# A bidirectional hybrid encoder on one core: sums of the twofold product moved to GpSimd, its first left operands split earlier, and a fixed order for the first matmuls

## The chip, the cores and the metric

The kernel runs on one core of one Trainium2 chip. The metric is the device time of one execution in microseconds. Three runs of the kernel before took 2148.56, 2149.13 and 2149.67 us, so the median is 2149.13 us. Engine names are those of the profile: PE is TensorE's matmul stream, PEld its weight loads, DVE is VectorE, ACT is ScalarE, POOL is GpSimd, SP is the sequencer that issues nearly all DMAs.

## What is computed

One encoder layer runs over 1,024 prompt tokens and 256 sample tokens, each with 16 meta tokens in front. All data are float32. Cut to what matters:

```python
u = rms_norm(h, norm_w) @ w_in            # 2048 -> 6656 columns: qa ka va za qb kb vb zb
ya = global_gqa(rope(norm(qa)), rope(norm(ka)), va) * silu(za)
yb = neighbourhood_attention(norm(qb), norm(kb), vb, rpb) * silu(zb)
y = concat([ya, yb]) @ w_out              # 2048 -> 2048
return h + y
```

## The kernel before

Every float32 product is made as three matmuls of split numbers. An operand is split into a high part, which ACT rounds (L72), and a low part, which DVE makes by subtracting the high part from the full number (L73). With high and low parts h and l, a product is h·h + h·l + l·h. The work has three stages: projection of a first token chunk (`chunk1`), projection and attention of the second (`chunk2`), and the output projection (`outproj`).

**The opening.** `strips` projects strips of 128 columns of `w_in`. The first call does three strips together: a key strip (j = 0), a value strip (j = 1) and a gate strip (j = 2, 496 columns where the others have 512). The contraction of 2,048 goes in 16 depth steps of 128, four of them to a chunk `c`. The list `OPENING` fixes for the first three chunks in which order inputs are loaded and split: a number is the x tile of a depth step (DMA L104, ACT L128, DVE L131), and a tuple is a strip's weights, or a range of depth steps of them, `(j, i, e)` (DMA L232, ACT L72, DVE L73). SP, ACT and DVE keep this order. The nine matmuls of a depth step (three products, lines L269, L270 and L271, for each strip) are only written in the order of the strips; the tile framework's scheduler places them on PE by its own estimate of when operands are ready. Ahead of them `chunk1` issues `WARM` matmuls on a zero tile (L692), on which nothing depends.

**The end of the attention and the output projection.** `outproj` makes the product with `w_out` by seven block products in place of eight. The first two, products 1 and 2, go in ten steps each: five token tiles t by two column halves, 24 matmuls a step (L1126 to L1128). In product 2 the step's result is added to a running tile by two DVE instructions, `o<-o,u` and `o<-o,pq` (L1136); the second reads PE's PSUM. The next block product is itself made by seven half-size products (`class Twice`): `GROUPS` lists 18 groups of 12 matmuls each (L1431), the first three for right operand "11" with token tiles 0, 1 and 4, the next three for "21", then t2, t3, t4, t1 and 22.

While PE does product 2, `Twice.ahead(n)` is called at each of its ten steps and prepares the first groups:

- `loads(2, n)` at steps 0 to 3 brings four tiles `ww` of 128x512 of each right operand, in the order "11", "21", "12", "22" (SP, L1093);
- `load_tile(t)` brings two tiles `yr` and `sum_tile(t)` adds them into `ysum` (128x1024, DVE, L1348);
- `weights(s)` makes the four sums of right operands t1 = 12 - 11, t2 = 22 - t1, t3 = 22 - 12 and t4 = 21 - t2, each as four DVE subtractions of 128x512 (L1348 too);
- `make(s)` splits right operands into `wm` (ACT L72, DVE L73); their slots are those of product 2's right operands, so each waits for PE to be done with the old one;
- `make_left(s, t)` splits a left operand into `yh` and `yl` (ACT L72, DVE L73).

From this stage on `in_order` ties each engine to the order in which the code is written, so a DVE or ACT instruction that waits holds all that stand behind it. In this order the splits of the first two left operands, ("11", 0) and ("11", 1), come last, at step 9, behind the splits `wm` of "11" and "21". POOL has no work after the attention.

Of the kernel before, what the change touches and what calls it, by code (L numbers as in the profile page):

```python
# [16 lines left out]
ALU = mybir.AluOpType  # L17
# [6 lines left out]
KT = 16  # L24
# [7 lines left out]
T1 = NMETA + NS + C1P  # L32
# [10 lines left out]
QB = 256  # L43
WIN0 = (0, 1, 3, 4)
HALF = 192
WARM = 7
WTYPE = (0, 1, 1, 2)
FILL = 1
LATE = 48
# [11 lines left out]
QA, KA, VA, ZA, QB_, KB, VB, ZB = 0, 8, 10, 12, 20, 28, 36, 44  # L61
# [4 lines left out]
class Kern:  # L66
# [146 lines left out]
    def strips(self, jobs, getx):  # L213


        nc, tc = self.nc, self.tc
        out = [[pool.tile([P, 512], F32, tag=tag, name="pp") for pool, tag in pools] for _, _, pools in jobs]
        for c in range(KT // WCH):
            behind = self.behind.pop(0) if self.behind else None
            ws = [None] * len(jobs)  # L220
# [29 lines left out]
            opening = self.projected == 3 and not self.second and c < len(OPENING)  # L250
# [4 lines left out]
                    piece(*o)  # L255
            nb = len(jobs[0][1])
            for b in range(nb)[::-1] if self.turn else range(nb):
                steps = [(j, c * WCH + k) for k in range(WCH) for j in range(len(jobs))]
                if self.projected > 50 and not self.second:
                    steps.sort()  # L260
                for j, kt in steps:
                    xh, xl = getx(kt)[b]
                    k, first, last = kt % WCH, kt == 0, kt == KT - 1
                    wh, wl, _ = ws[j]
                    p, n = out[j][b], jobs[j][1][b][1]
                    if (jobs[j][0], c) in self.wide:
                        n = T1
                    m = T1 if first and jobs[j][0] == QA + 2 and not self.second else n
                    nc.tensor.matmul(p[:, :m], wh[:, k, :], xh[:, :m], start=first, stop=False)  # L269
                    nc.tensor.matmul(p[:, :n], wh[:, k, :], xl[:, :n], start=False, stop=False)  # L270
                    self.lastmm = nc.tensor.matmul(p[:, :n], wl[:, k, :], xh[:, :n], start=False, stop=last).ins  # L271
# [395 lines left out]
                yield  # L667

    def chunk1(self):
        self.opening = [None, None]  # L670
# [666 lines left out]
class Twice:  # L1337
# [26 lines left out]
    def weights(self, s):  # L1364
# [40 lines left out]
    def ahead(self, n):  # L1405
        if n < 4:
            self.loads(2, n)
        for f, x in {2: [(self.load_tile, 0)], 3: [(self.load_tile, 1)], 4: [(self.sum_tile, 0)],
                     5: [(self.load_tile, 4), (self.sum_tile, 1), (self.weights, "t1")],
                     6: [(self.load_tile, 2), (self.weights, "t2")],  # L1410
                     7: [(self.sum_tile, 4), (self.load_tile, 3), (self.weights, "t3"), (self.weights, "t4")],
                     8: [(self.sum_tile, 2), (self.make, "11"), (self.make, "21")]}.get(n, ()):
# [168 lines left out]
```

## Time and profile before

| what | number |
|---|---|
| median of three runs | 2149.13 us |
| the profiled execution's own time | 2149.74 us |
| its span, first to last instruction | 2148.0 us |
| PE busy | 2139.4 us, 100% |
| DVE, ACT, POOL busy | 1699.2, 1218.5, 539.4 us |
| PE's waits for other engines, all added | 5.0 us |
| from the start of product 2's last step to its end | 1867.99 to 1873.4 us |
| groups of the twofold product | from 1873.4 us |

Times inside the execution count from the start of the span. A timeline row gives the start, the busy time, the engine, the line, the operation and its tiles, how many instructions the row merges (x4), and in brackets how long the engine had been idle before it and what ended that idle time. PE's ends are modelled: its matmuls overlap, so their rate is read from one start to the next. A window row gives each engine's busy time with its instruction count, then the granted TensorE clock (1.00 is full speed), the DMA share and the bytes moved.

### The profile page before, as it was taken

The numbers are of one execution on the slowest core, as the hardware profiler recorded it, in microseconds if no ns is written. First come the engines' busy times: TensorE is split into PE (matmuls) and PEld (weight loads), VectorE is DVE, ScalarE is ACT, GpSimd is POOL, SyncE is SP. The second block draws the span as 40 slices with busy tenths as digits, with TensorE's granted clock in tenths as the row PEclk, the third lists the DMA queues.
The fourth block names the chain that finished last, engine by engine and source line by source line (L and its number), as shares of the span: only waits on it lengthen the run. The fifth ranks groups of instructions, "written<-read, shape, count | busy, mean of one in ns | idle before, by whom it ended". The sixth has DMA issues, their size and how long they took to land.

```text
span 2148.0 us, 33409 instructions
## 1 busy us (share of the span) xinstructions
PE 2139.4 (100%) x11437; PEld 1862.2 (87%) x11437; DVE 1699.2 (79%) x3103; ACT 1218.5 (57%) x2470; POOL 539.4 (25%) x250
## 2 busy tenths in 40 slices
PE   9999999999999999999999999999999999999999
PEld 7888888888888889998998888999989988788887
DVE  7798877777874899898799888787787776686763
ACT  7777644555665777777677776444444454262230
POOL 1242422233221223232133413333333312000000
PEclk9999999999999999999999999999999999999999
DMA  8757799987654333334333333654434355852663
GB/s 295 224 184 227 246 319 308 338 280 265 213 187 131 101 104 113 102 106 125 101 103 101 106 119 126 209 161 137 131 128 125 115 193 183 288 163 97 235 225 108
DMA packets 257707, 377.21 MB, mean 176 GB/s; under 512 B 43104, under 2 KB 109184, under 8 KB 257536
## 3 DMA queue, kind: packets, MB, share of 16 engines
q1 hardware_dynamic: 256960, 374.80, 54.0%
q8 instruction: 90, 1.47, 0.3%
q14 instruction: 81, 0.66, 0.1%
q10 hardware_dynamic: 576, 0.27, 0.0%
HBM read 281.01 MB, written 100.38 MB: 178 GB/s over the span
## 4 chain that ended last, share of the span: by engine, by line
PE 97%; DVE 1%; DMA 1%; SPq 0%; issue 0%; ACT 0%; DVEq 0%; ACTq 0%
PE pp L271 22%; PE pp L269 22%; PE pp L270 22%; PE pq L1128 4%; PE pq L1126 4%; PE pq L1127 4%; PE po L464 3%; PE pq L1431 2%; PE po L564 2%; PE sp L530 2%; PE sp L424 2%; PE sp L425 2%; PE sp L426 2%; PE po L465 1%; PE tp L585 0%; DMA yl<-yd 0%
## 5 line engine op out<-in xcount | busy, mean ns | idle before, releaser
L269 PE MATMUL pp<-x,wh 128*128 128x512 f32 (+1 forms) x1664 | 651.3, 394 | 0.6 <-ACT wh L72 0.6
L271 PE MATMUL pp<-x,wl 128*128 128x512 f32 (+1 forms) x1664 | 647.3, 389 | 0.7 <-DVE wl L73 0.7
L270 PE MATMUL pp<-x,wh 128*128 128x512 f32 (+1 forms) x1664 | 646.7, 389 | 0.0
L271 PEld LDWEIGHTS pp<-x,wl 128*128 128x128 f32 x1664 | 312.4, 188 | 64.3 <-DVE wl L73 1.8
L269 PEld LDWEIGHTS pp<-x,wh 128*128 128x128 f32 x1664 | 312.6, 188 | 55.4 <-ACT wh L72 2.1
L270 PEld LDWEIGHTS pp<-x,wh 128*128 128x128 f32 x1664 | 312.7, 188 | 54.1 <-DVE x L131 0.3
L304 POOL PARTITION_ALL_REDUCE m<-ms x78 | 238.4, 3056 | 297.7 <-ACT ms L302 207.3
L388 POOL PARTITION_ALL_REDUCE tot<-a x80 | 182.1, 2276 | 462.4 <-DVE a L385 429.8
L73 DVE TENSOR_TENSOR wl<-wr,wh 128x512 fp32r<-128x512 f32 (+2 forms) x288 | 210.1, 734 | 89.1 <-ACT wh L72 68.5
L72 ACT CAST wh<-wr 128x512 fp32r<-128x512 f32 (+2 forms) x288 | 173.8, 609 | 166.4 <-PE pp L270 150.7
L270 PE MATMUL pp<-xb,wh 128*128 128x272 f32 x832 | 240.4, 289 | 0.0
L269 PE MATMUL pp<-xb,wh 128*128 128x272 f32 x832 | 239.5, 288 | 0.0
L271 PE MATMUL pp<-xb,wl 128*128 128x272 f32 x832 | 239.2, 288 | 0.0
L370 POOL PARTITION_ALL_REDUCE ma<-m x80 | 112.3, 1403 | 452.8 <-DVE m L368 439.8
L1126 PE MATMUL pq<-wm,yh 128*128 128x512 f32 x480 | 187.5, 391 | 0.0
L1127 PE MATMUL pq<-wm,yh 128*128 128x512 f32 x480 | 186.9, 389 | 0.0
L1128 PE MATMUL pq<-wm,yl 128*128 128x512 f32 x480 | 186.8, 389 | 0.0
L270 PEld LDWEIGHTS pp<-xb,wh 128*128 128x128 f32 x832 | 156.4, 188 | 8.5
L269 PEld LDWEIGHTS pp<-xb,wh 128*128 128x128 f32 x832 | 156.5, 188 | 8.1
L271 PEld LDWEIGHTS pp<-xb,wl 128*128 128x128 f32 x832 | 157.4, 189 | 0.9
L73 DVE TENSOR_TENSOR ph<-S,ph 128x512 fp32r<-128x512 f32 x136 | 101.7, 755 | 13.5 <-ACT ph L72 13.2
L1128 PEld LDWEIGHTS pq<-wm,yl 128*128 128x128 f32 x480 | 90.1, 188 | 18.7
(241 smaller groups left out, 3996.4 us busy)
## 6 DMA issues: line engine op xcount, KB each, us to landing
wr<-in_w_in SPq DMA_DIRECT2D x413, 256.0 KB, 3.5
wld<-wl SPq DMA_DIRECT2D x132, 256.0 KB, 4.3
wl<-wld SPq DMA_DIRECT2D x132, 256.0 KB, 3.2
yr<-yd SPq DMA_DIRECT2D x35, 512.0 KB, 4.8
wq<-in_w_out SPq DMA_DIRECT2D x64, 256.0 KB, 4.8
td<-wq SPq DMA_DIRECT2D x64, 256.0 KB, 3.3
ww<-td SPq DMA_DIRECT2D x64, 256.0 KB, 4.4
ww<-in_w_out SPq DMA_DIRECT2D x48, 256.0 KB, 4.7
```

Source lines behind the costliest of these rows:

```text
L72: self.hi = nc.scalar.copy(hi, full).ins
L73: return nc.vector.tensor_tensor(out=lo, in0=full, in1=hi.bitcast(F32), op=ALU.subtract).ins
L269: nc.tensor.matmul(p[:, :m], wh[:, k, :], xh[:, :m], start=first, stop=False)
L270: nc.tensor.matmul(p[:, :n], wh[:, k, :], xl[:, :n], start=False, stop=False)
L271: self.lastmm = nc.tensor.matmul(p[:, :n], wl[:, k, :], xh[:, :n], start=False, stop=last).ins
L304: nc.gpsimd.partition_all_reduce(m2[:], ms[:], P, RED.add)
L370: nc.gpsimd.partition_all_reduce(ma[:], m1[:], P, RED.max)
L388: nc.gpsimd.partition_all_reduce(tot[:], a1[:], P, RED.add)
L464: nc.tensor.matmul(po[:], vh, hl[:, i], start=j == 0, stop=False)
L1126: nc.tensor.matmul(ps, yh, wh, start=k == 0, stop=False)
L1127: nc.tensor.matmul(ps, yh, wl, start=False, stop=False)
L1128: self.lastmm = nc.tensor.matmul(ps, yl, wh, start=False, stop=k == 7).ins
```

## The change

Five edits:

1. `Twice.weights` issues its sixteen subtractions on GpSimd instead of VectorE.
2. `Twice.ahead` calls `make_left("11", 0)` and `make_left("11", 1)` at step 8, ahead of `sum_tile(2)` and of the splits of "11" and "21", instead of at step 9 behind them.
3. In the first chunk (c == 0) of the opening a list `FIRST` gives the order of the nine matmuls of a depth step as pairs (strip, product), one list for the first depth step and one for the next three, and each matmul is placed behind the one before.
4. `OPENING` takes the x tile of depth step 2 ahead of the second halves of the weights of strips 1 and 2.
5. `WARM` goes from 7 to 8.

```diff
-WARM = 7
+WARM = 8
-OPENING = ([0, (0, 0, 1), (1, 0, 2), (2, 0, 2), (0, 1, 2), 1, (0, 2, 4), (1, 2, 4), (2, 2, 4), 2, 3],
+OPENING = ([0, (0, 0, 1), (1, 0, 2), (2, 0, 2), (0, 1, 2), 1, (0, 2, 4), 2, (1, 2, 4), (2, 2, 4), 3],
+FIRST = [[(int(c), int(q)) for c, q in o.split()] for o in ("00 10 01 02 11 12 20 21 22", "00 10 20 01 02 11 12 21 22")]
@@ strips
-                steps = [(j, c * WCH + k) for k in range(WCH) for j in range(len(jobs))]
-                if self.projected > 50 and not self.second:
+                steps = [(j, c * WCH + k, (0, 1, 2)) for k in range(WCH) for j in range(len(jobs))]
+                if opening and c == 0:
+                    steps = [(j, k, (q,)) for k in range(WCH) for j, q in FIRST[k > 0]]
+                elif self.projected > 50 and not self.second:
                     steps.sort()
...
+                    for q in products:
...
+                        i = nc.tensor.matmul(out[j][b][:, :m], w[q // 2][:, k, :], x[q % 2][:, :m], start=first, stop=last).ins
+                        if opening and c == 0 and self.lastmm:
+                            self.place_after(i, self.lastmm, "in turn")
+                        self.lastmm = i
@@ Twice.weights
-            self.sub(out[i], self.raw[a][i], self.raw[b][i])
+            self.nc.gpsimd.tensor_tensor(out=out[i], in0=self.raw[a][i], in1=self.raw[b][i], op=ALU.subtract)
@@ Twice.ahead
-                     8: [(self.sum_tile, 2), (self.make, "11"), (self.make, "21")]}.get(n, ()):
-            f(x)
-        if n == 9:
-            self.make_left("11", 0)
-            self.make_left("11", 1)
+                      8: [(self.make_left, "11", 0), (self.make_left, "11", 1), (self.sum_tile, 2), (self.make, "11"), (self.make, "21")]}.get(n, ()):
+            f(*x)
```

All instructions outside these two places keep their order on every engine. Line numbers move by one to three: L269 to L271 become one line, L271, and L72, L73, L1136 and L1348 become L73, L74, L1139 and L1351.

On PE, at the start of the program, the names pp_347, pp_348 and pp_349 are the sums of strips 0, 1 and 2 in the kernel before, x_350 and x_374 the x tiles of depth steps 0 and 1 (high or low part), and wh and wl the weights' parts:

```order
L269 MATMUL pp_347<-x_350,wh_354 128x512
L269 MATMUL pp_348<-x_350,wh_359 128x512
L269 MATMUL pp_349<-x_350,wh_365 128x496
L270 MATMUL pp_347<-x_350,wh_354 128x512
L270 MATMUL pp_348<-x_350,wh_359 128x512
L270 MATMUL pp_349<-x_350,wh_365 128x496
L271 MATMUL pp_347<-x_350,wl_355 128x512
L271 MATMUL pp_348<-x_350,wl_360 128x512
L269 MATMUL pp_347<-x_374,wh_354 128x512
L269 MATMUL pp_348<-x_374,wh_359 128x512
L271 MATMUL pp_349<-x_350,wl_366 128x496
```

The same place now, where the strips' sums are pp_348, pp_349 and pp_350 and the x tiles x_351 and x_375:

```order
L271 MATMUL pp_348<-x_351,wh_355 128x512
L271 MATMUL pp_349<-x_351,wh_360 128x512
L271 MATMUL pp_348<-x_351,wh_355 128x512
L271 MATMUL pp_348<-x_351,wl_356 128x512
L271 MATMUL pp_349<-x_351,wh_360 128x512
L271 MATMUL pp_349<-x_351,wl_361 128x512
L271 MATMUL pp_350<-x_351,wh_366 128x496 x2
L271 MATMUL pp_350<-x_351,wl_367 128x496
L271 MATMUL pp_348<-x_375,wh_355 128x512
L271 MATMUL pp_349<-x_375,wh_360 128x512
```

Strip 2's first product, the third matmul before, now stands seventh; the four products of strips 0 and 1 with low parts have moved ahead of it. On SP the DMA of the x tile of depth step 2 has moved ahead of two weight DMAs (128x256 each); ACT and DVE each handle that x tile ahead of the second half of strip 1's weights.

On DVE, from step 7 of product 2 to the preparations for the third group, before:

```order
L1348 TENSOR_TENSOR ww<-ww 128x512 x4
L1348 TENSOR_TENSOR wt<-ww,v 128x512 x4
L1136 TENSOR_TENSOR o<-o,u 128x512
L1136 TENSOR_TENSOR o<-o,pq 128x512
L1348 TENSOR_TENSOR ysum<-yr 128x1024
L73 TENSOR_TENSOR wm<-ww,wm 128x512 x8
L1136 TENSOR_TENSOR o<-o,u 128x512
L1136 TENSOR_TENSOR o<-o,pq 128x512
L73 TENSOR_TENSOR yl<-ysum,yh 128x512 x2
L1136 TENSOR_TENSOR o<-o,u 128x512
L1136 TENSOR_TENSOR o<-o,pq 128x512
L73 TENSOR_TENSOR wm<-v,wm 128x512 x4
```

The same stretch now:

```order
L1139 TENSOR_TENSOR o<-o,u 128x512
L1139 TENSOR_TENSOR o<-o,pq 128x512
L74 TENSOR_TENSOR yl<-ysum,yh 128x512 x2
L1351 TENSOR_TENSOR ysum<-yr 128x1024
L74 TENSOR_TENSOR wm<-ww,wm 128x512 x8
L1139 TENSOR_TENSOR o<-o,u 128x512
L1139 TENSOR_TENSOR o<-o,pq 128x512
L1139 TENSOR_TENSOR o<-o,u 128x512
L1139 TENSOR_TENSOR o<-o,pq 128x512
L74 TENSOR_TENSOR wm<-v,wm 128x512 x4
```

The sums are gone from DVE (the first eight stand higher up in the same way), and the two `yl` of the first left operands stand ahead of `ysum` and of the eight `wm`. On ACT the two `yh` of those operands have moved ahead of the eight `wm` in the same way. On POOL, behind its last reduction of the attention, now stand one instruction that the order lists as `ISA` (L1378, with no wait; the same kind stands ahead of POOL's first select and its first reduction) and the sixteen subtractions, in the order t1, t2, t3, t4.

More of the change, by code (lines that the diff above doesn't have):

```diff
@@ L257, in strips @@
             for b in range(nb)[::-1] if self.turn else range(nb):
-                steps = [(j, c * WCH + k) for k in range(WCH) for j in range(len(jobs))]
-                if self.projected > 50 and not self.second:
+                steps = [(j, c * WCH + k, (0, 1, 2)) for k in range(WCH) for j in range(len(jobs))]
+                if opening and c == 0:
+                    steps = [(j, k, (q,)) for k in range(WCH) for j, q in FIRST[k > 0]]
+                elif self.projected > 50 and not self.second:
                     steps.sort()
[L261 to L271, printed above, removed]
+                for j, kt, products in steps:
+                    x = getx(kt)[b]
+                    k, w = kt % WCH, ws[j]
+                    n = T1 if (jobs[j][0], c) in self.wide else jobs[j][1][b][1]
+                    for q in products:
+                        first, last = kt == q == 0, kt == KT - 1 and q == 2
+                        m = T1 if first and jobs[j][0] == QA + 2 and not self.second else n
+                        i = nc.tensor.matmul(out[j][b][:, :m], w[q // 2][:, k, :], x[q % 2][:, :m], start=first, stop=last).ins
+                        if opening and c == 0 and self.lastmm:
+                            self.place_after(i, self.lastmm, "in turn")
+                        self.lastmm = i
                 if self.turned and (c, b) == self.tie:
```

10 lines of the change are left out of this document (5 added, 5 removed).

## The prediction

> **What bounds the kernel now.** I read the page's first line and PE's waits first.
>
> ```profile
> span 2148.0 us, 33409 instructions
> ```
>
> ```profile
> PE pq L1431 <- DVE yl L73: 2.5, 1, 2.5
> PE warm L692 <- DVE wz L689: 1.2, 1, 1.2
> PE pp L271 <- DVE wl L73: 0.7, 1, 0.7
> PE pp L269 <- ACT wh L72: 0.6, 2, 0.3
> ```
>
> PE is busy all the time but for four waits of 5.0 us together, in 2148 us. So this change, which takes no matmul away, can win little. Half of the waiting is one wait at the head of the twofold product, where the change works; the last row is the opening, where it works too. The timeline of PE and the windows around the first place come next.
>
> ```profile
> 1867.99 0.39 PE L1126 MATMUL pq<-wm,yh 128*128 128x512 f32 x1
> ...
> 1873.43 0.61 PE L1431 MATMUL pq<-wm,yh 128*128 128x512 f32 x2
> 1876.52 0.79 PE L1431 MATMUL pq<-wm,yl 128*128 128x512 f32 x1 [2.47 <-DVE yl L73]
> ...
> 1880.20 0.39 PE L1431 MATMUL pq<-wm,yl 128*128 128x512 f32 x1
> ```
>
> ```profile
> 1873.00:1876.50 3.50, 1.04 (x5) 0.54 (x3) 3.47 (x7) 0.00 (x0) 0.00 (x0) 0.99 0.86 291
> 1876.50:1880.20 3.70, 3.69 (x9) 2.94 (x10) 3.60 (x7) 0.00 (x0) 0.00 (x0) 0.55 0.91 295
> ```
>
> The last step of product 2 takes 24 matmuls from 1867.99 to 1873.43, which is 0.227 us each. Two matmuls of the twofold product follow, then PE is idle for 2.47 us. What the list of waits doesn't show stands in the second window: behind the wait the granted clock is 0.55, and from 1876.52 to 1880.20 nine matmuls take 3.68 us where nine at 0.227 take 2.04. The wait thus costs 2.47 + 1.64 = 4.11 us.
>
> Who made the wait stands in DVE's timeline.
>
> ```profile
> 1849.98 1.31 DVE L73 TENSOR_TENSOR yl<-yl,yh 128x512 fp32r<-128x512 f32 x2 [2.86 <-ACT yh L72]
> ...
> 1852.34 2.49 DVE L1348 TENSOR_TENSOR v<-ww 128x512 f32<-128x512 f32 x4
> ...
> 1864.69 2.49 DVE L1348 TENSOR_TENSOR wt<-ww,v 128x512 f32<-128x512 f32 x4
> ...
> 1869.63 4.90 DVE L73 TENSOR_TENSOR wm<-ww,wm 128x512 fp32r<-128x512 f32 x8
> ...
> 1875.78 1.28 DVE L73 TENSOR_TENSOR yl<-ysum,yh 128x512 fp32r<-128x512 f32 x2
> ```
>
> From 1849.98 on DVE hardly pauses. Four groups of four sums lie in that stretch, each holding it for about 2.4 us (instructions of 0.68 us that start 0.60 apart): 9.6 us. The `yl` that PE waits for begins at 1875.78, behind all of them and behind the eight `wm`.
>
> **The change part by part: the sums and the splits.** Without the sums DVE has no backlog. ACT sets the new pace.
>
> ```profile
> 1863.43 5.38 ACT L72 CAST wm<-ww 128x512 fp32r<-128x512 f32 x8 [4.88 <-PE pq L1128]
> ```
>
> The second left operand's slot comes free when step 7 ends, 5.44 us ahead of 1867.99, at 1862.6, so ACT splits it by about 1863.3 and the `wm` follow from 1863.9 to 1868.1 or so; the edit costs ACT some 0.4 us there. The two `yl` are then done by 1864.6. With `ysum` (1.1) and eight `wm` (4.8) DVE stands at 1870.5, with three of the four o instructions behind (0.6 each) at 1872.3, and it now waits for PE's step 9 (1873.6). PE needs the first `yl` at 1873.9 and has had it for 9 us. The gain at this place is 4.11 us.
>
> What is late next: the operands of the following groups, since PE reaches them 4.1 us earlier. A group takes 12 × 0.227 = 2.72 us, so ("11", 4) needs its `yl` at 1873.43 + 5.44 + 0.45 = 1879.3. DVE starts from PE's end of step 9, 1873.9, with o<-o,pq (0.6), four `wm` (2.4) and this `yl` (0.6): 1877.5, with 1.8 us to spare. Two groups later the same sum (`ysum`, two splits, two sums of 1.1 each, two `wm`) gives 1883.3 against 1884.8. I take no new wait.
>
> The sums on POOL: sixteen operations that the trace doesn't show on that engine. The nearest rows are these.
>
> ```profile
> 9.75 0.28 POOL masks.py:199 TENSOR_SCALAR_AFFINE_SELECT ident<-ident 128x128 f32<-128x128 f32 x1 [8.19 <-issue]
> ...
> 1796.51 2.01 POOL L388 PARTITION_ALL_REDUCE tot<-a  x1 [2.88 <-DVE a L385]
> ```
>
> ```profile
> L304 POOL PARTITION_ALL_REDUCE m<-ms x78 | 238.4, 3056 | 297.7 <-ACT ms L302 207.3 <-issue 43.4 <-DVE rs_r L93 26.0
> ```
>
> An operation with one input on a quarter of the elements took 0.28, so 1.1 us for 128x512 is the lower bound; the reduction over partitions on up to 128x512, 3.06, the upper. I take 1.1 to 1.2, nearest to the plain elementwise row. They can start when tiles of "12" and "22" are there.
>
> ```profile
> 1830.51 1.80 SPq L1093 DMA_DIRECT2D ww<-td x4
> ```
>
> ```profile
> 1834.53 7.16 DMA ww<-td
> ```
>
> "12" is issued from 1830.51; the chain of waits has one tile of "22" on its way from 1834.53 for 7.16 us, to 1841.7. If "12" takes as long, it lands from 1837.7 at the latest. At 1.1 us the sums end by 1855 to 1863; their first reader on ACT, the split of t2, stands behind the `wm`, at about 1868. Cover of 5 us or more; at 3.06 us the eight sums of t1 and t2 would still be done by 1837.7 + 24.5 = 1862. The idle 8.19 us ahead of the select, which I read as setting POOL up, may come again ahead of the sums; POOL's last work ends at 1798.5 and the sums have their data nearly 40 us later, so it is hidden, and uncovered it would only shift the sums by 8 us. The loads of the next right operands wait in SP's queue for the readers of the old ones, the sums among them, and hold the stores and loads behind them; before, the last of these readers were the eight `wm`, done at 1874.5 (1869.63 + 4.90), so sums that end sooner add nothing there.
>
> The Trainium skill, "GPSIMD Engine Reference", section 3.1, gives 4497 ns for such an operation on 2,048 elements, so by estimate 1.1 us for 512; no run here shows it yet.
>
> **The clock.** A rule speaks against part of my sum. The row above has the clock at 0.55 behind 2.47 us of idleness. The Trainium skill, "TensorE: Matmul & The Clock Gate", Part 1, says that the clock falls back after at least one idle window of about 3.4 us, and its summary warns of gaps over some 3 us. By that the gap is too short, only 2.47 us would be won here, and the total would be 2146.8. The trace decides: nine matmuls in 3.68 us.
>
> **The change part by part: the opening.**
>
> ```profile
> 1.17 3.17 PE L692 MATMUL warm<-wz 128*128 128x512 bf16 x7 [1.17 <-DVE wz L689]
> 4.64 1.22 PE L269 MATMUL pp<-x,wh 128*128 128x512 f32 x2 [0.31 <-ACT wh L72]
> 6.14 0.49 PE L269 MATMUL pp<-x,wh 128*128 128x496 f32 x1 [0.27 <-ACT wh L72]
> ...
> 9.89 0.84 PE L269 MATMUL pp<-x,wh 128*128 128x512 f32 x3
> ```
>
> ```profile
> 5.68 0.60 ACT L72 CAST wh<-wr 128x256 fp32r<-128x256 f32 x2 [0.78 <-DMA wr<-in_w_in]
> ...
> 8.90 0.72 ACT L128 ACTIVATE x<-xr,nw 128x512 fp32r<-128x512 f32 x1 [0.95 <-DMA xr<-in_x]
> ```
>
> ```profile
> 5.06 0.62 DVE L73 TENSOR_TENSOR wl<-wr,wh 128x128 fp32r<-128x128 f32 x2
> ```
>
> The third matmul waits for strip 2's weights, which land at 5.68, until 6.14. In the new order the low parts of strips 0 and 1 fill this time: their `wl` are done at 5.68, the low x part before. The second matmul starts near 5.23; then one follows at 5.66 and one near 6.0 (the first ones come 0.43 apart, as the seven on zeros do) and from there every 0.227. Nine are issued by 7.4, and nine more bring depth step 2 to 9.44 instead of 9.89: 0.45 us won. Its x tile was split from 8.90 to 9.6 and would be late; edit 4 sends that DMA ahead of two others on SP, and these two hold as many bytes as the tile: by estimate it comes nearly 1 us earlier and the second halves of strips 1 and 2 that much later, near 9, just in time. So edits 3 and 4 are worth 0.45 us, with bounds of +0.7 and -0.45 (the wait stays and as much is added at depth step 2, where every matmul now stands behind the one before). The eighth matmul on zeros would start at 4.16 and free PE at about 4.6; the first real one waits until 4.64: nothing, at most 0.1.
>
> **The sum.** 4.11 + 0.45 = 4.56 us off the profiled execution's own 2149.74 (span 2148.0) is 2145.2. That execution is 0.61 us above the median of the runs; part of their spread of 1.1 us must be the length and the aftermath of the gap, which goes, and the rest I count at a third, 0.2: 2145.0. Against 2149.13 that is 4.1 us or 0.19%. What a measurement of this kernel can tell from no change is about 0.2%, 4.3 us: the forecast lies on that edge. Its own range is 2144.2 to 2145.8.
>
> **Rivals.** First, POOL's sums hold up DVE, and the kernel gets slower. For it speak these rows (nanoseconds, shortest, middle and longest; and one of them in DVE's timeline).
>
> ```profile
> L397 DVE TENSOR_TENSOR tot<-tot,r x80: 403/425/1870, 132.0 to 1799.5; 128x256 f32<-128x256 f32 x80
> ```
>
> ```profile
> 1796.90 1.21 DVE L397 TENSOR_TENSOR tot<-tot,r 128x256 f32<-128x256 f32 x1
> ```
>
> An operation with two SBUF inputs of 0.425 us took up to 1.87, and one of 1.21 began at 1796.90, within POOL's reduction from 1796.51; most of the 80 were not slowed, which speaks against. Suppose that a sum and such a DVE instruction always exclude each other. Until 1863 DVE has only some 8 us of them, and sums of 1.1 us, each giving way, end near 1863 (1841.7 + 12 × 1.1 + 8): harmless. At 2.1 us each they end at 1875; from 1863 DVE then gets 0.6 us of work in every 2.7, is 9.4 us behind, and 6.5 after its slack of 1.2 and 1.8. With a slow clock behind it (1.64) that is 2145.0 + 8.1 = 2153. It decides from about 1.75 us a sum, where the loss equals the gain. The Trainium skill, "SBUF — State Buffer", Who interferes with whom, states such an exclusive lock for a VectorE instruction with two SBUF inputs against a GpSimd one that reads SBUF. By that rule this is the case, and only the sums' length decides. Chance 7%.
>
> Second, the same in a milder form: DVE reaches ("11", 4) about 1 us late, and a new wait of 1 us with its slow clock takes the place of the old: 2145.0 + 2.6 = 2147.6. For it speaks that DVE's slack is just 1.8 us there; against it, that the sums should be over by then. Chance 10%.
>
> Third, the fixed order in the opening does not do what it says: depth step 2 waits for the late weight halves, 0.45 us are lost instead of won: 2145.0 + 0.9 = 2145.9. DMA is at its limit there (a tile's landing ends ACT's idle time at 8.90). Chance 11%.
>
> **How the numbers follow.** The forecast has 72%, of which 40 lie beyond 0.2% and 32 within. Faster by over 0.2%: 40%. Within 0.2%: 32 + 10 + 11 = 53%. Slower: 7%. The range takes in the second and third rivals and leaves the first out: up to 2148.0. Down it takes 0.25 for a better opening, 0.4 for the rest of the 0.61 and the 0.5 that another wait (L271, 0.7 us) could lose: 2143.8.
>
> **What would show it.** Right: no wait of PE at L1431, a clock of 1.00 from 1870 to 1885, the two `yl<-ysum` on DVE before 1866, sums on POOL of about 1.1 us that end before 1864, and depth step 2 at about 9.4. Wrong: a wait on `wm` or `yl` at a later group, DVE instructions of twice their length beside POOL's, sums above 1.75 us, or a wait in the first 12 us longer than 0.3. A run over 2149 would refute the forecast altogether.

## The result and the profile after

| | before | after |
|---|---|---|
| median of 20 runs each | 2148.92 us (2146.75 to 2150.70) | 2145.40 us (2144.55 to 2146.52) |
| the profiled execution's own time | 2149.74 us | 2145.56 us |
| its span | 2148.0 us | 2143.4 us |

The ratio is 0.9984, 95% interval 0.9978 to 0.9990: the change saves 3.5 us, 0.16%. That is less than the 0.2% the prediction called measurable; with twenty runs on each side the interval still excludes 1. The forecast was 2145.0 in a range of 2143.8 to 2148.0.

The profile of the changed kernel begins with its span and the busy times.

```profile
span 2143.4 us, 33426 instructions
...
PE 2137.6 (100%) x11438; PEld 1861.2 (87%) x11438; DVE 1700.1 (79%) x3087; ACT 1218.6 (57%) x2470; POOL 564.5 (26%) x266
```

POOL has gained 25 us of work, and DVE has not lost any: its sixteen sums are gone (9.6 us), and still its busy time is 0.9 us higher than before. PE's list of waits, which had 5.0 us in four rows, now has two rows.

```profile
PE warm L695 <- DVE wz L692: 1.2, 1, 1.2
PE pp L271 <- ACT x L129: 0.5, 1, 0.5
```

The wait of 2.47 us at the head of the twofold product is gone. PE's timeline there has no brackets, and the window around it (busy time of PE, PEld, DVE, ACT and POOL, then the granted clock, DMA share and GB/s) shows PE full at clock 1.00 where the second window of before had 0.55.

```profile
1872.84 0.62 PE L1431 MATMUL pq<-wm,yh 128*128 128x512 f32 x2
1873.29 0.39 PE L1431 MATMUL pq<-wm,yl 128*128 128x512 f32 x1
1873.52 0.62 PE L1431 MATMUL pq<-wm,yh 128*128 128x512 f32 x2
```

```profile
1870.00:1885.00 15.00, 15.00 (x68) 12.43 (x67) 14.83 (x22) 8.63 (x17) 0.00 (x0) 1.00 0.53 174
```

DVE's timeline shows why. The two `yl` that PE waited for come at 1863.81 instead of 1875.78, and the one of the third group (last row) is done at 1876.8.

```profile
1863.81 1.29 DVE L74 TENSOR_TENSOR yl<-ysum,yh 128x512 fp32r<-128x512 f32 x2
...
1866.15 4.90 DVE L74 TENSOR_TENSOR wm<-ww,wm 128x512 fp32r<-128x512 f32 x8
...
1873.68 2.49 DVE L74 TENSOR_TENSOR wm<-v,wm 128x512 fp32r<-128x512 f32 x4
1876.09 0.68 DVE L74 TENSOR_TENSOR yl<-ysum,yh 128x512 fp32r<-128x512 f32 x1
```

POOL's timeline has the sixteen sums, four to a row.

```profile
1833.38 5.95 POOL L1378 TENSOR_TENSOR v<-ww 128x512 f32<-128x512 f32 x4 [35.07 <-ACT yh L73]
1841.70 5.87 POOL L1378 TENSOR_TENSOR v<-ww,v 128x512 f32<-128x512 f32 x4 [2.38 <-DMA ww<-td]
1847.53 5.93 POOL L1378 TENSOR_TENSOR ww<-ww 128x512 f32<-128x512 f32 x4
1853.43 7.39 POOL L1378 TENSOR_TENSOR wt<-ww,v 128x512 f32<-128x512 f32 x4
```

By these rows a sum takes 1.47 to 1.49 us (5.87/4 to 5.95/4), the last four 1.85, and the last ends at 1860.8. The rows mix two lengths, though, as the shortest, middle and longest sum show (nanoseconds):

```profile
L1378 POOL TENSOR_TENSOR v<-ww,v x4: 1290/1483/1744, 1841.7 to 1846.3; 128x512 f32<-128x512 f32 x4
L1378 POOL TENSOR_TENSOR wt<-ww,v x4: 1742/1750/2272, 1853.4 to 1859.1; 128x512 f32<-128x512 f32 x4
```

A sum that meets no two-input DVE instruction takes 1.29 us; beside one it takes 1.74, and beside the larger `ysum` 2.27. What DVE does beside them is slowed too, and in one pattern.

```profile
1838.10 1.78 DVE L1139 TENSOR_TENSOR o<-o,u 128x512 f32<-128x512 f32 x1
1840.40 0.69 DVE L1139 TENSOR_TENSOR o<-o,pq 128x512 f32<-128x512 f32 x1 [0.53 <-PE pq L1131]
...
1849.57 2.75 DVE L74 TENSOR_TENSOR yl<-yl,yh 128x512 fp32r<-128x512 f32 x2 [3.04 <-ACT yh L73]
```

`o<-o,u`, with both inputs in SBUF, takes 1.78 us where it took 0.69 before; `o<-o,pq`, whose second input is in PSUM, stays at 0.69; two `yl` take 2.75 instead of 1.31.

The opening, on PE and then on ACT:

```profile
1.17 3.33 PE L695 MATMUL warm<-wz 128*128 128x512 bf16 x8 [1.17 <-DVE wz L692]
4.58 1.03 PE L271 MATMUL pp<-x,wh 128*128 128x512 f32 x3
...
7.44 1.28 PE L271 MATMUL pp<-x,wh 128*128 128x512 f32 x4 [0.47 <-ACT x L129]
...
9.70 1.09 PE L271 MATMUL pp<-x,wh 128*128 128x512 f32 x4
```

```profile
6.66 0.72 ACT L129 ACTIVATE x<-xr,nw 128x512 fp32r<-128x512 f32 x1 [0.59 <-DMA xr<-in_x]
7.61 0.73 ACT L129 ACTIVATE x<-xr,nw 128x512 fp32r<-128x512 f32 x1
```

The two waits on weights have gone. A new one of 0.47 us stands ahead of depth step 1, whose x tile lands only at 6.66; that of depth step 2, sent earlier, is split at 7.61, long before its use. Depth step 2 begins at 9.70, 0.19 us sooner than in before's profile.

**Where the 4.6 us of span came from.** The twofold product starts at 1872.84, 0.59 us sooner than before's 1873.43. The opening gives 0.19 of that. A wait of PE for `wl` near 584 us (the 0.7 in before's list), which this run doesn't have and which the change doesn't touch, gives more than the rest; some of it is lost again before the twofold product. From the start of the twofold product to the end of the span it is now 270.6 us (2143.4 - 1872.84) where it was 274.6 (2148.0 - 1873.43): 4.0 us. So the change has a hand in 4.2 of the 4.6.

Two costs stand against this. From the start of PE's last matmul (2144.07, now 2139.17) the span goes on for 4.2 us instead of 3.9; up to that matmul, the twofold product and what follows it became 4.3 us shorter. And the execution's own time fell by 4.18 us and not by 4.6: 2.16 us of it (2145.56 - 2143.4) lie outside the span, where 1.74 did. The second cost is in every run of the kernels with the sums on POOL but those of e9 (2.1 to 2.3 us), and in none of the others whose span is on record (1.7 to 1.9). No run shows what causes either.

### The profile page after: what moved, and what is told of

The parts are those of the page before. It is cut to its first block, busy times and chain, and to the rows that moved or that the text cites. A ratio compares the mean times of both kernels' runs of the same rounds, so it can differ in the third digit from the quotient of the medians.

```text
span 2143.4 us, 33426 instructions
## 1 busy us (share of the span) xinstructions
PE 2137.6 (100%) x11438; PEld 1861.2 (87%) x11438; DVE 1700.1 (79%) x3087; ACT 1218.6 (57%) x2470; POOL 564.5 (26%) x266
## 3 DMA queue, kind: packets, MB, share of 16 engines
q8 instruction: 90, 1.47, 0.3%
## 4 chain that ended last, share of the span: by engine, by line
PE 98%; DVE 1%; DMA 0%; issue 0%; SPq 0%; ACT 0%; DVEq 0%
PE pp L271 66%; PE pq L1130 5%; PE pq L1131 5%; PE pq L1129 5%; PE po L467 3%; PE pq L1431 2%; PE sp L533 2%; PE po L567 2%; PE sp L427 2%; PE sp L428 2%; PE sp L429 2%; PE po L468 2%; PE tp L588 0%; PE sm_ps L361 0%; PE sm_ps L360 0%
## 5 line engine op out<-in xcount | busy, mean ns | idle before, releaser
L271 PE MATMUL pp<-x,wh 128*128 128x512 f32 (+1 forms) x3328 | 1037.9, 391 | 0.5 <-ACT x L129 0.5
L271 PEld LDWEIGHTS pp<-x,wh 128*128 128x128 f32 x3328 | 610.2, 188 | 109.0 <-ACT wh L73 0.9
L271 PE MATMUL pp<-x,wl 128*128 128x512 f32 (+1 forms) x1664 | 647.5, 389 | 0.1
L271 PEld LDWEIGHTS pp<-x,wl 128*128 128x128 f32 x1664 | 312.4, 188 | 63.4 <-DVE wl L74 0.9
L271 PE MATMUL pp<-xb,wh 128*128 128x272 f32 x1664 | 334.2, 288 | 0.0
L271 PEld LDWEIGHTS pp<-xb,wh 128*128 128x128 f32 x1664 | 276.1, 188 | 16.6
L74 DVE TENSOR_TENSOR wl<-wr,wh 128x512 fp32r<-128x512 f32 (+2 forms) x288 | 211.1, 737 | 87.6 <-ACT wh L73 64.9
L73 ACT CAST wh<-wr 128x512 fp32r<-128x512 f32 (+2 forms) x288 | 174.0, 609 | 163.8 <-PE pp L271 151.2
L271 PE MATMUL pp<-xb,wl 128*128 128x272 f32 x832 | 239.2, 288 | 0.0
L271 PEld LDWEIGHTS pp<-xb,wl 128*128 128x128 f32 x832 | 157.4, 189 | 0.9
L74 DVE TENSOR_TENSOR ph<-S,ph 128x512 fp32r<-128x512 f32 x136 | 101.9, 756 | 13.2 <-ACT ph L73 12.9
L1129 PEld LDWEIGHTS pq<-wm,yh 128*128 128x128 f32 x480 | 90.1, 188 | 18.6
L1130 PEld LDWEIGHTS pq<-wm,yh 128*128 128x128 f32 x480 | 90.1, 188 | 18.5
L447 DVE TENSOR_TENSOR S<-S,ma 128x512 f32<-128x512 f32 x136 | 94.6, 750 | 8.9 <-POOL ma L373 8.9
L89 ACT ACTIVATE rs_l<-m 128x512 f32<-128x512 f32 (+1 forms) x78 | 43.7, 561 | 100.4 <-DVE m L308 99.7
```

The source lines that it names most:

```text
L73: self.hi = nc.scalar.copy(hi, full).ins
L74: return nc.vector.tensor_tensor(out=lo, in0=full, in1=hi.bitcast(F32), op=ALU.subtract).ins
L89: nc.scalar.activation(l[:], ms, AF.Ln)
L271: i = nc.tensor.matmul(out[j][b][:, :m], w[q // 2][:, k, :], x[q % 2][:, :m], start=first, stop=last).ins
L447: nc.vector.tensor_tensor(out=s, in0=s, in1=mb, op=ALU.subtract)
L1129: nc.tensor.matmul(ps, yh, wh, start=k == 0, stop=False)
```

## The experiments

**Theory:** DVE's backlog of sums makes the gap. On POOL the sums are far enough ahead, the gap goes, and with it the half clock behind it. **Rivals:** moving the left operands forward is enough; the sums on POOL hold DVE up and are safe only by their small number; the opening is where the gain comes from. Each kernel's time is compared with runs of the kernel before on the same chip.

### Only the sums on POOL (e1)

```diff
-            self.sub(out[i], self.raw[a][i], self.raw[b][i])
+            self.nc.gpsimd.tensor_tensor(out=out[i], in0=self.raw[a][i], in1=self.raw[b][i], op=ALU.subtract)
```

> The kernel before with edit 1 alone: the sixteen sums on GpSimd, the first two left operands still split at step 9, the old opening. My theory (DVE's backlog of 9.6 us of sums made the gap): the first yl is ready near 1871.6, before PE comes to it at 1873.9, so no wait at L1431 and no slow clock; about 2145.7 us, 3.2 less than before's median of 2148.9. Rival (the earlier place of the splits is what counts): a wait of 1 us or more stays at the head of the twofold product; 2147 us or more.

Measured: 2146.15 us against 2148.53, ratio 0.9986 (0.9977 to 0.9995). The time lies between the two expectations, 0.45 above the theory's; the wait decides between them. PE has none at L1431. The `yl` still stand behind the `wm`, but they start 3.6 us sooner than before, and PE's third matmul there, at 1874.23 (0.45 behind the start at 1873.78), finds the first one done. This is DVE's row:

```profile
1872.18 1.29 DVE L73 TENSOR_TENSOR yl<-ysum,yh 128x512 fp32r<-128x512 f32 x2
```

So edit 1 alone removes the gap; edit 2 is not needed for it.

### Only the left operands first (e2)

This kernel has edit 2 alone: the two `make_left` at step 8 ahead of `sum_tile(2)`, and the sums on DVE.

```diff
-                     8: [(self.sum_tile, 2), (self.make, "11"), (self.make, "21")]}.get(n, ()):
+                      8: [(self.make_left, "11", 0), (self.make_left, "11", 1), (self.sum_tile, 2), (self.make, "11"), (self.make, "21")]}.get(n, ()):
```

> The kernel before with edit 2 alone: the first two left operands split at step 8, the sums still on VectorE. My theory: the two yl and the first four wm are just in time for group 0, but DVE's backlog stays and the yl of (11, 4) comes near 1881, some 1.8 us after PE needs it, so the wait moves to the third group and shrinks only a little; 2147.5 to 2148.9 us. Rival (the order is what counts): no wait, about 2145.7 us, as the whole change.

Measured: 2147.98 us, ratio 0.9994 (0.9985 to 1.0003). PE's timeline shows that the wait has moved to the third group; the two windows are the wait and the stretch behind it.

```profile
1880.69 0.50 PE L1428 MATMUL pq<-wm,yl 128*128 128x512 f32 x1 [1.72 <-DVE yl L73]
```

```profile
1878.30:1880.70 2.40, 0.68 (x4) 0.22 (x3) 2.40 (x5) 2.14 (x4) 0.00 (x0) 1.00 0.80 195
1880.70:1884.10 3.40, 3.40 (x15) 2.83 (x16) 3.37 (x4) 0.81 (x2) 0.00 (x0) 1.00 0.71 244
```

As expected: the order alone moves the wait, the backlog stays. The clock stayed at 1.00 behind 1.72 us.

### Both at the product, with the old opening (e3)

Edits 1 and 2 as shown above, edits 3 to 5 undone.

> Edits 1 and 2 together with the old opening. My theory: the gap and its slow clock are gone, and only the opening's 0.2 to 0.4 us are missing against the whole change: 2145.6 to 2145.8 us. Rival (the opening earned a good part): 2146.5 us or more.

Measured: 2147.01 us, ratio 0.9991 (0.9983 to 1.0000), so the rival's number. The profile (span 2146.8) has no gap at the twofold product, but this in the opening:

```profile
11.86 0.95 PE L269 MATMUL pp<-x,wh 128*128 128x512 f32 x3 [2.02 <-ACT x L128]
```

With the old order the x tile of depth step 2 can come 2 us late. From here on all of PE's work stands that much later: the twofold product starts at 1876.20, and from there to the span's end it is the same 270.6 us as after the whole change. A late opening now reaches the end in full.

### The gap filled with other matmuls (e6)

The kernel before, with eight extra matmuls ahead of the one that waits. They write a tile that nobody reads.

```diff
+                if g == i == 0 and a is yl:
+                    fill = k.sp.tile([P, 2, QB], F32, tag="sp", name="fill")
+                    for _ in range(8):
+                        nc.tensor.matmul(fill[:].rearrange("p a b -> p (a b)"), yh[:, 0, :], wm[:, 0, :], start=True, stop=True)
```

> The kernel before, with eight more matmuls on operands already there (their result is used by nothing) put into the gap, between the second and the third matmul of group 0. They take 1.8 of its 2.47 us. My theory (the half clock behind the gap comes from PE's own idleness): the third matmul still waits for its yl until 1876.5, but the clock stays at 1.00 and the next nine matmuls take 2.04 us and not 3.68: 1.6 us less in the profile, 1 to 1.6 us less in the median, 2147.3 to 2147.9. Rival (the clock drops there for another reason, or a gap shorter than 3.4 us does not count and other runs have no slow clock): no difference, 2148.9.

Measured: 2147.86 us against 2148.53, ratio 0.9996 (0.9987 to 1.0005), so no change that can be told. PE's timeline, and the windows of the gap and of what follows:

```profile
1874.61 1.98 PE L1434 MATMUL fill<-wm,yh 128*128 128x512 f32 x8
1876.53 0.50 PE L1435 MATMUL pq<-wm,yl 128*128 128x512 f32 x1
```

```profile
1873.00:1876.60 3.60, 3.60 (x17) 2.70 (x15) 3.56 (x7) 0.18 (x1) 0.00 (x0) 1.00 0.73 230
1876.60:1880.30 3.70, 3.70 (x17) 3.05 (x18) 3.60 (x7) 1.18 (x3) 0.00 (x0) 1.00 0.94 304
```

Behind the gap seventeen matmuls now fit into 3.70 us, where nine did, at clock 1.00. And the third matmul of the group starts at 1876.53, as in before's profile (1876.52), although PE arrived 0.72 us later (its first at 1874.15, for 1873.43): the end of the gap is set by DVE's chain and not by PE. In this pair of profiles the gap swallowed what the opening lost.

### Only the opening (e4)

Edits 3 to 5 alone, as in the diff of the change.

> The kernel before with edits 3, 4 and 5 alone: the whole new opening, the sums and splits as before. My theory after the first runs (the end of the gap at 1876.5 is set by DVE's chain, which starts with a landing near 1849 and not with PE, so PE's delays in the opening are swallowed by the gap): PE comes to the gap up to 1 us earlier and waits that much longer; the median stays within 0.5 us of before's 2148.5. Rival (the opening's gain stands on its own): 2147.3 to 2147.8 us.

Measured: 2146.66 us against 2148.31, ratio 0.9993 (0.9984 to 1.0002). That meets neither expectation as it was written, though the interval includes no change. The gap is there, shorter:

```profile
1876.39 0.50 PE L1434 MATMUL pq<-wm,yl 128*128 128x512 f32 x1 [1.93 <-DVE yl L74]
```

The clock behind it is 1.00. A half clock that did not come explains little of the 1.65 us: among the runs at full clock alone, the medians are 2146.56 and 2148.15. That speaks against a gap that simply swallows what the opening won, but as the interval includes no change, it stays open; and the profiled execution, at 2148.16, was one of this kernel's longest.

### The sums made twice (e5)

The changed kernel, with each sum issued twice (those of t3 three times), 36 instead of 16; the results are the same numbers.

```diff
-            self.nc.gpsimd.tensor_tensor(out=out[i], in0=self.raw[a][i], in1=self.raw[b][i], op=ALU.subtract)
+            for _ in range(3 if s == "t3" else 2):
+                self.nc.gpsimd.tensor_tensor(out=out[i], in0=self.raw[a][i], in1=self.raw[b][i], op=ALU.subtract)
```

> The changed kernel with every sum on GpSimd issued twice, and those of t3 (made in place) three times: 36 instructions of 1.47 us and more in place of 16, the same result. Theory (a sum and a VectorE instruction with two SBUF inputs exclude each other): the sums last until 1886 or later, DVE gets one such instruction per sum from 1863 on and is 10 us or more behind at the third group; 2154 to 2162 us, slower than before. Rival (no exclusion; DVE's longer instructions beside the sums cost nothing by themselves): t2 is done near 1857, t3 near 1875, both before their readers, and the time stays within 1 us of the changed kernel, 2145 to 2146.5.

Measured: 2164.07 us, ratio 1.0069 (1.0053 to 1.0084), a little beyond the theory's 2162. PE's longest waits, then DVE and POOL where they meet:

```profile
PE pq L1432 <- DVE yl L74: 13.4, 1, 13.4
PE pq L1432 <- DVE wm L74: 1.9, 3, 0.7
```

```profile
1870.86 13.62 DVE L74 TENSOR_TENSOR wm<-ww,wm 128x512 fp32r<-128x512 f32 x8
```

```profile
1859.07 21.50 POOL L1379 TENSOR_TENSOR ww<-ww 128x512 f32<-128x512 f32 x12
1880.52 13.42 POOL L1379 TENSOR_TENSOR wt<-ww,v 128x512 f32<-128x512 f32 x8
```

Eight `wm` take 13.62 us instead of 4.90, 1.70 each, and a sum beside them 1.79 (21.50/12): the two engines take turns, one instruction each (21.50 us are twelve sums, some of them ahead of the `wm`). This is the first rival's mechanism, at the first rival's place. In the change the sums end at 1860.8, ahead of the `wm`, and so it costs nothing.

### One edit of the opening at a time (e7, e8)

e7 is edits 1, 2 and 4: the x tile of depth step 2 early, no fixed order of matmuls, seven warm ones. e8 is the change without edit 4:

```diff
-OPENING = ([0, (0, 0, 1), (1, 0, 2), (2, 0, 2), (0, 1, 2), 1, (0, 2, 4), 2, (1, 2, 4), (2, 2, 4), 3],
+OPENING = ([0, (0, 0, 1), (1, 0, 2), (2, 0, 2), (0, 1, 2), 1, (0, 2, 4), (1, 2, 4), (2, 2, 4), 2, 3],
```

> Edits 1, 2 and 4: the sums and splits of the change, and of the new opening only the earlier x tile of depth step 2; no set order of matmuls. Theory (what the new opening does is to take away a wait of 0 to 2 us for that x tile, which the gap used to swallow): no wait longer than 0.3 us at depth step 2, a median of 2145.3 to 2146.0 and a small spread. Rival (the set order does it): 2146.5 or more, as edits 1 and 2 alone.

> The changed kernel without edit 4: the x tile of depth step 2 in its old place, the matmuls in the set order and the eighth matmul on zeros. Theory: PE comes to depth step 2 about 0.4 us earlier and waits there for the x tile, 0.4 to 2.4 us; a median of 2146.3 to 2147.2, as edits 1 and 2 alone. Rival (the set order is what counts): 2145.4.

Measured: e7 2146.06 us, ratio 0.9990 (0.9981 to 0.9999); e8 2145.62, ratio 0.9986 (0.9977 to 0.9995). The start of depth step 2, in e7 and then in e8:

```profile
9.85 0.86 PE L269 MATMUL pp<-x,wh 128*128 128x512 f32 x3
```

```profile
10.12 1.28 PE L271 MATMUL pp<-x,wh 128*128 128x512 f32 x4 [0.51 <-ACT x L129]
```

In each the expected wait is there or not there as the theory had it. But e8's time misses the theory's 2146.3 to 2147.2 and comes near the rival's, and e7's lies 0.06 us above its own, with runs from 2145.19 to 2148.62 and not the small spread. The two times can't be told apart by their intervals, so which of the opening's edits earns what stays open.

### The next x tile earlier still (e9)

```diff
-OPENING = ([0, (0, 0, 1), (1, 0, 2), (2, 0, 2), (0, 1, 2), 1, (0, 2, 4), 2, (1, 2, 4), (2, 2, 4), 3],
+OPENING = ([0, (0, 0, 1), (1, 0, 2), 1, (2, 0, 2), (0, 1, 2), 2, (0, 2, 4), (1, 2, 4), (2, 2, 4), 3],
```

> The changed kernel with the x tile of depth step 1 loaded and split one place earlier, ahead of strip 2's first weights, and that of depth step 2 right behind strip 0's low parts. Theory (the only wait left in the opening is the 0.47 us for x of depth step 1, and its DMA comes in the order of issue): that wait is gone, the three matmuls on strip 2's weights wait a little instead, depth step 2 begins 0.1 to 0.4 us sooner than 9.70, and the time is that of the changed kernel less 0 to 0.4 us, 2145.0 to 2145.6, which no median here can tell from it. Rival (DMA is at its limit in the opening, and what comes sooner makes its neighbour come later by as much): depth step 2 begins at 9.7 or after, time 2145.4 to 2146.

Measured: 2145.57 us, ratio 0.9986 (0.9977 to 0.9995).

```profile
7.37 0.72 PE L271 MATMUL pp<-x,wh 128*128 128x496 f32 x2 [0.80 <-ACT wh L73]
...
10.58 1.09 PE L271 MATMUL pp<-x,wh 128*128 128x512 f32 x4
```

The wait for x is gone, strip 2's weights come 0.80 us late instead, and depth step 2 begins 0.88 us later than in the change's profile: the rival, by the trace; the time fits both expectations. The DMA share is 0.92 to 0.95 from 2 to 10 us in this profile, so a tile that comes sooner can make its neighbour late; here a wait of 0.47 us went and one of 0.80 came.

### Both kernels profiled again (e10, e11)

> The kernel before, unchanged, profiled a second time. Theory (the gap at the head of the twofold product ends where DVE's chain sets it, and the half clock behind it depends on how long PE was idle): PE waits 1.5 to 2.5 us for yl there and its third matmul starts near 1876.5, however late PE arrives; x of depth step 2 may come up to 2 us late, and that delay is swallowed by the gap. A half clock only if the wait is again above 2 us. Rival (the half clock was chance): a wait above 2.3 us with the clock at 1.00 behind it.

> The changed kernel, unchanged, profiled a second time. Theory: no wait in the output projection, clock 1.00 from 1870 to 1885, POOL's sums again 1.4 to 1.9 us each, a wait of 0.2 to 0.8 us for x of depth step 1 in the opening and none at depth step 2. Rival (the landing of x tiles in the opening varies from run to run in this order too): a wait above 0.8 us in the opening, which then shows in full in the span, as no gap behind it swallows it.

The kernel before took 2147.87 us in this run (span 2146.1), the changed one 2144.65 (span 2142.5). The gap of before, and the window behind it:

```profile
1876.08 0.50 PE L1431 MATMUL pq<-wm,yl 128*128 128x512 f32 x1 [2.19 <-DVE yl L73]
```

```profile
1876.50:1880.20 3.70, 3.70 (x18) 3.05 (x17) 3.60 (x7) 1.52 (x3) 0.00 (x0) 1.00 1.00 292
```

The gap came again, with the same cause, and the half clock did not: the theory's threshold of 2 us of waiting did not hold. The gap ends 0.44 us sooner than in the first profile, with DVE's chain, whose `yl` starts at 1875.34 instead of 1875.78. The changed kernel again has no wait in the output projection, and POOL's sums again take 1.4 to 1.9 us each by their rows. The expected wait of 0.2 to 0.8 us in the opening did not come, nor did the rival's longer one; depth step 2 begins about when it did:

```profile
9.77 1.09 PE L271 MATMUL pp<-x,wh 128*128 128x512 f32 x4
```

### Two counts over all runs

**How often the clock falls.** Half the clock for 3.41 us (its length in the clock records of before's first profile) lowers the mean granted clock of a run to 0.999. That mean is on record for each run. Beside the experiments the kernel before ran 75 times:

| mean clock | runs of before | median |
|---|---|---|
| 1.000 | 46 | 2148.03 us |
| 0.999 | 24 | 2149.61 us |
| 0.998 | 5 | 2152.33 us |

So a lowered clock comes in 29 of 75 runs, and where it comes once the run is 1.58 us longer by the medians; the prediction had worked out 1.64. Where in a run it lay is on record only for the profiled ones. But of the 11 runs with the gap filled (e6) none shows it, and none of the 76 runs of kernels without the gap: 20 and 1 of the changed kernel, 11 each of e1, e3, e7, e8 and e9. With the wait moved to the third group (e2) it was 2 of 11, with the opening alone (e4) 1 of 11, and with 13.4 us of waiting (e5) 4 of 4.

**From the twofold product to the end.** Spans and starts, in us, are those of the profiles; x1 and x2 stand for the x tiles of depth steps 1 and 2. The last column is the span less the start of the twofold product:

| kernel | depth step 2 starts | PE's wait at the first or third group | twofold product starts | span | difference |
|---|---|---|---|---|---|
| before | 9.89 | 2.47, half clock behind | 1873.43 | 2148.0 | 274.6 |
| before again (e10) | 9.83 | 2.19 | 1873.28 | 2146.1 | 272.8 |
| left operands only (e2) | 9.77 | 1.72 | 1872.92 | 2145.7 | 272.8 |
| gap filled (e6) | 10.46 | filled | 1874.15 | 2146.5 | 272.4 |
| opening only (e4) | 9.82 | 1.93 | 1873.85 | 2146.4 | 272.6 |
| sums only (e1) | 10.02 | none | 1873.78 | 2144.3 | 270.5 |
| old opening (e3) | 11.86 | none | 1876.20 | 2146.8 | 270.6 |
| x2 early (e7) | 9.85 | none | 1873.32 | 2143.9 | 270.6 |
| no x2 early (e8) | 10.12 | none | 1872.88 | 2143.5 | 270.6 |
| x1 earlier (e9) | 10.58 | none | 1873.62 | 2144.2 | 270.6 |
| after | 9.70 | none | 1872.84 | 2143.4 | 270.6 |
| after again (e11) | 9.77 | none | 1871.91 | 2142.5 | 270.6 |

Without the gap the rest of the program is 270.5 to 270.6 us in every kernel, so by the span the gap costs 4.0 us with the half clock and 1.8 to 2.2 without. Both would be some 0.35 us more without the longer end behind PE's last matmul, which all kernels in the rows without a gap have.

## Why the prediction was right

**The gap: right in the mechanism, and its price is paid only in some runs.** The prediction put 2.47 us of waiting and 1.64 us of slow clock on L1431, 4.11 together; in the profiled execution 4.3 went on PE, and 4.0 by the span. e1 shows that the sums made the gap, e2 that the order of the splits alone only moves it, and e6 that idleness makes the slow clock: with the gap filled it is in none of 11 runs. But 1.64 us is the price of a run in which the clock falls, and that is 29 of 75. In the other 46 the gap costs its own length, 2.2 us in e10, and so the median gain of 3.5 is below the 4.6 of the two profiles.

**From the profiled execution to the median: the adjustment fits, and a term is missing.** For the step from the profiled execution to the median the text took 0.2 us, and the changed kernel's median lies 0.16 below its profiled execution (2145.40 and 2145.56). The sum's own result for that execution, 2145.2, is 0.4 too low, and as much time was added outside the span (1.74, now 2.16), which the sum put at nothing. The gain in the medians, 3.5 from before's 2148.92 where the text has 4.1, is smaller for that reason too. That the sum of 4.56 meets the 4.6 of span is luck: 4.11 became 4.0, 0.45 became 0.19, and the rest came from a wait near 584 us that the text had only in its lower bound ("another wait (L271, 0.7 us)"). The text's reading that PE is busy "all the time but for four waits" also leaves out the 3.5 us behind its last matmul, which is where the change lost 0.35.

**The operands that come next: right.** `yl` of the first groups were forecast by 1864.6 and are done at 1865.1 (1863.81 + 1.29). The third group's was forecast for 1877.5 against a need at 1879.3; it is done at 1876.8 (1876.09 + 0.68), and PE, which started 0.59 sooner, needs it at 1878.7. There is no new wait; the second rival did not come.

**The sums: a term mis-sized, without effect.** They were taken at 1.1 to 1.2 us and take 1.29 alone and 1.74 beside a two-input DVE instruction, 1.57 in the mean (25.14/16). The prediction chose the plain elementwise row of 0.28 us for a quarter of the elements and multiplied by four; the bounds of 1.1 and 3.06 held. The end, forecast for 1855 to 1863, is 1860.8, because they start at 1833.4, before the 1837.7 that was allowed for. The 1.1 us that "GPSIMD Engine Reference", section 3.1, of the Trainium skill gives by estimate is too short here as well.

**The first rival: its mechanism is real, its condition was not met.** DVE instructions of 128x512 with two SBUF inputs take up to 1.78 us beside a sum, with one of them in PSUM 0.69. The Trainium skill states this lock ("SBUF — State Buffer", Who interferes with whom), and the traces agree. The rival put the point of decision at 1.75 us a sum, and the mean was 1.57. e5 did not make the sums longer but more, so that they ran on to 1893.9 (1880.52 + 13.42, POOL's last row), and gave 2164: the cover is real and ends where the `wm` begin. The change has 5.3 us of it (1866.15 - 1860.8).

**The opening: the forecast missed its term.** 0.45 us were forecast and depth step 2 at 9.44; it came at 9.70 and 9.77. The step that failed is "nine are issued by 7.4, and nine more bring depth step 2 to 9.44": PE had issued the first nine by 6.8, sooner than forecast, but then waited for the x tile of depth step 1, and the first four matmuls from 7.44 on take 1.12 us instead of 0.91. No line of the sum had looked at that tile: it lands at 6.66. On the other side the edits earn something that the sum didn't have. In the profiles with the old order of loads and matmuls depth step 2 began at 9.77 to 11.86 us (before, e1, e2, e3, e6, e10); with its x tile early (after, e4, e7, e11) at 9.70 to 9.85. Without the gap that scatter reaches the end (e3). By the ratios of e1 and e3 (0.9986 and 0.9991) against the change's 0.9984 the opening would be worth 0.4 to 1.5 us, and by e4's runs at full clock 1.6; but these intervals overlap, so the size stays open, and so does which of edits 3 to 5 brings it. The third rival (depth step 2 waits for late weights) did not come: in the change nothing waits there. Only e9 has a wait on late weights, at the first depth step and by another order of loads.

**The signs of being wrong.** Three that the prediction named came: DVE instructions of twice their length beside the sums (1.78 for 0.69), sums above 1.75 us (the last four, 1.85), and a wait above 0.3 in the first 12 us (0.47). None touched the main term, because the first two ended ahead of the `wm` and the third cost 0.26 (9.70 for 9.44).

**The clock rule.** By "TensorE: Matmul & The Clock Gate", Part 1, of the Trainium skill, the clock falls after at least one idle window of about 3.4 us, and the windows run on regardless of the kernel. Gaps of 1.72, 1.93 and 2.19 us left it at 1.00 in the profiles of e2, e4 and e10; one of 2.47 us did not. So a whole idle window isn't needed, against the page. The clock records show where the windows stand: in all thirteen profiles the times between two changes of the clock are whole multiples of 3.413 us (before has full clock for 548 of them, up to 1876.43, then half for one). Here is PE's busy time in the window that holds before's gap and in the next one, then in the window that holds most of e10's gap:

```profile
1873.02:1876.43 3.41, 1.02 (x5) 0.52 (x3) 3.38 (x7) 0.00 (x0) 0.00 (x0) 1.00 0.87 294
1876.43:1879.84 3.41, 3.33 (x8) 2.65 (x9) 3.31 (x7) 0.00 (x0) 0.00 (x0) 0.50 0.90 299
```

```profile
1874.35:1877.77 3.42, 1.69 (x7) 1.43 (x8) 3.28 (x6) 0.00 (x0) 0.00 (x0) 1.00 0.87 285
```

Before's gap lies nearly whole in one window, 2.39 us of it idle, and the clock falls at its end; e10's is divided between two, 1.73 in the one shown. The end of e7, where PE runs out of work, is nearest to the border among the windows with a fall, that of e1 among those without:

```profile
2138.64:2142.05 3.41, 1.40 (x7) 0.82 (x5) 0.75 (x2) 0.00 (x0) 0.00 (x0) 1.00 0.20 70
2142.05:2143.90 1.85, 0.00 (x0) 0.00 (x0) 0.00 (x0) 0.00 (x0) 0.00 (x0) 0.50 0.04 13
```

```profile
2138.86:2142.27 3.41, 1.64 (x8) 1.02 (x6) 0.75 (x2) 0.00 (x0) 0.00 (x0) 1.00 0.12 43
2142.27:2144.30 2.03, 0.00 (x0) 0.00 (x0) 0.00 (x0) 0.00 (x0) 0.00 (x0) 1.00 0.16 57
```

In all thirteen profiles the full clock fell at the end of every window with 2.01 us or more of idle PE, and of none with 1.77 or less. So what counts is not the length of the gap alone but how much of it falls into one window, and one kernel can come out on both sides. For the runs without a profile this is argued from the profiles.

Not settled: waits of PE outside the change that come in some profiles and not in others (`wl` near 584 us, 0.7 in before and none in after; `S` in the attention, up to 1.1 in e3), the spread of before's runs at full clock, 2145.46 to 2151.02, and the longer end of the kernels with sums on POOL.

## What to carry to other kernels

A short idle stretch of PE can cost more than its length, but not in every run: before a single profile's half clock goes into a sum, count in how many runs the mean clock is below 1. A span isn't the whole execution: compare the executions' own times as well. Work moved from DVE to POOL is not free of DVE: ask which two-input SBUF instructions run at the same time, and whether the last moved one ends before DVE's work is on the critical path. A gap whose end another engine sets can swallow a delay ahead of it, as in e6's profile, though e4's runs speak against that as a rule; once it is gone, those delays count.

## What the runs showed of the hardware

- A subtraction of 128x512 float32 on POOL takes 1.29 us when no DVE instruction with two SBUF inputs runs and 1.74 beside one of 128x512; such a DVE instruction takes 1.70 to 1.78 us in turn with the sums, where it took 0.61 to 0.69.
- An idle stretch of 2.47 us was enough to halve TensorE's granted clock for 3.41 us, and one of 2.19 in the same kernel was not. The clock changed only at borders 3.413 us apart, and fell where PE had been idle for 2.01 us or more between two of them, but not at 1.77 or less.
- The idle 8.19 us ahead of POOL's first select in before are gone in the kernels with the sums on POOL: there the select begins at 1.86 or 1.87 us, 0.30 behind POOL's last instruction; in the others it begins at 9.1 to 10.4. Whether POOL idles like that ahead of the sums can't be seen, as it has nothing to do for 35 us before 1833.38.
